# Gate logits of a gated DeltaNet layer as float32 products in four column groups, and its first decay rows spread by TensorE

## The chip, the core and the metric

The kernel runs on one core of one Trainium2 chip. The core has a matrix engine (TensorE, PE in the rows), a vector engine (VectorE, DVE), a scalar engine (ScalarE, ACT), GpSimd (POOL) and a queue that issues DMA transfers (SyncE, SP). Each engine works through its own instructions in a fixed order and waits on semaphores for the others. The metric is the device time of one execution in microseconds; lower is better.

## The reference

A prompt of 512 tokens and 8 groups of 4 sample tokens go through two layers; each layer is half an FFN, a mixer, and half an FFN, all on one residual stream. The second (odd) layer's mixer is a gated DeltaNet. Cut to what the change touches:

```python
def macaron_layer(x, mixer, n1, w1i, w1o, nm, n2, w2i, w2o):
    x = x + 0.5 * swiglu(rms_norm(x, n1), w1i, w1o)
    m, new_state = mixer(rms_norm(x, nm))
    x = x + m
    return x + 0.5 * swiglu(rms_norm(x, n2), w2i, w2o), new_state

def deltanet_mixer(u, conv_buf, S0, w_in, conv_w, A_log, dt_bias, o_gain, w_out):
    proj = u @ w_in                       # 1024 x 4112: q, k, v, z (1024 each), 8 + 8 logits
    qkv, z, b_logit, a_logit = jnp.split(proj, [...], axis=-1)
    qkv, new_buf = causal_conv(conv_buf, qkv, conv_w)
    q, k, v = jnp.split(jax.nn.silu(qkv), 3, axis=-1)     # 8 heads of 128, q and k normalized
    beta = jax.nn.sigmoid(b_logit)
    g = -jnp.exp(A_log) * jax.nn.softplus(a_logit + dt_bias)
    o, S = gated_delta_chunked(q, k, v, beta, g, S0)
    ...

def gated_delta_chunked(q, k, v, beta, g, S0):
    G = jnp.cumsum(gc, axis=-1)                           # within a chunk
    decay = jnp.exp(jnp.where(incl, G[..., :, None] - G[..., None, :], -jnp.inf))
    A = jnp.where(strict, jnp.einsum('bnhcd,bnhsd->bnhcs', kc, kc) * decay, 0.0) * bc[..., None]
    sol = lax.linalg.triangular_solve(A, rhs, ...)
    P = jnp.einsum('bnhcd,bnhsd->bnhcs', qc, kc) * decay
    ...                                                   # then a scan over the chunks
```

## The kernel before

The residual stream lies turned: 8 tiles x[k] of 128 features by 544 tokens (512 of the prompt, 32 samples), in float32. Beside each stands a pair xh, xl: the tile times the norm's gain, split in a rounded part and its rest. A large product (`mm3`, lines 367 to 369) is three products of such parts, wh xh + wh xl + wl xh, added up in an accumulator "lin" over the 8 feature tiles, once for 256 tokens and once for 288. Of "lin" there are two in the odd mixer. The norm's factor rstd is multiplied in only when VectorE empties the accumulator, so the products need not wait for the norm. A weight tile (`W`) is loaded by SP into one of two "raw" buffers, split by ScalarE (wh, line 328, three buffers) and VectorE (wl, line 329, two buffers).

The odd mixer begins with `norm_stats`: the sums of squares over the features are products with a matrix of ones (lines 288, 289), and rstd follows on ScalarE and VectorE. Then `odd_setup` makes beta and g for all tokens and heads. The 16 logits are a `mm3` with a weight of 16 columns: 48 products with 16 output rows. VectorE multiplies by rstd (bt, line 1043), TensorE turns bt to tokens by logits with five transposes (line 1047), and some twenty small VectorE instructions make g (line 1065). Products with triangles of ones sum it up to G (lines 1070 to 1074). G is turned once more (line 1098), copied (gt), written to DRAM (gdr) in five transfers, and read back into all partitions: grs for the samples (line 1105) and one "grow" per head (line 1160). `head_decay` makes from grow two decay matrices per head, Dn and Dt, in 16 VectorE instructions for two heads and some exponentials.

`odd_heads` works off a list of steps (`ODD_ORDER`, line 955): D decays, H the conv tiles of q and k and the products of a head (`head_stage`), B its values, V the triangular solve of two heads on VectorE (`solve`), Z the gate, L the levels that join the solved blocks (`levels`), C the chain over the chunks (`chain`), S and R the samples, O and M the output products. Two heads form a group. A conv tile (`conv_tile`) is one `mm3`, whose result VectorE copies times rstd into XP (lines 1120, 1123, 1124) and convolves in one ScalarE and three VectorE passes (lines 1132, 1134). `head_stage` squares q and k on ScalarE only for the sums; the squares themselves go to a scratch tile "junk". The tiles Dn, Dt, kt, qg and vb of all groups share 15 buffers of tag "st", in turn; accumulators of tag "m" are two.

A scheduler derives the order of each engine from the program and the dependences, and the whole odd mixer is ordered together; where instructions stand can be read only from the built program. `E.after` adds a dependence for the order alone.

## Time and profile before

| | us |
|---|---|
| median of 3 runs | 1911.97 (1911.93 to 1913.39) |
| the profiled execution | 1916.94 |
| its span, first to last instruction | 1915.2 |
| TensorE busy | 1861.2 (97%) |
| VectorE busy | 1078.1 (56%) |
| ScalarE busy | 836.9 (44%) |
| mean granted clock of TensorE | 0.991 of 2.4 GHz |

The profile is of one execution. Times within it count from the span's start. The last FFN of the layer ahead ends near 1197 us and the odd mixer fills the time to about 1610 us. Products are pipelined: one shown as 0.29 us starts 0.12 to 0.13 us behind the one ahead, at the full clock.

### The profile page before, as it was taken

The page shows a single profiled execution, that of the slowest core. Times are in us where ns is not written, and L with a number is a line of the kernel's source. Part 1 is how long each engine was busy: PE and PEld are TensorE (multiplying, and loading weights), DVE is VectorE, ACT ScalarE, POOL GpSimd, SP SyncE. Part 2 cuts the span into 40 slices and gives each one's busy share as a digit, 9 for nine tenths or more (in the row PEclk, how much of TensorE's full clock was granted, in tenths as well). Part 3 has the DMA queues.
Part 4 walks back from the last instruction along what each step waited for, and adds up shares of the span by engine and source line. Part 5 has one row for each costly group of instructions (what it writes and reads, how often), then busy time and mean ns, then how long its engine had stood idle before and what let it go on. Part 6 is the DMA issues. An engine that isn't in the chain of part 4 may idle for free.

```text
span 1915.2 us, 36694 instructions
## 1 busy us (share of the span) xinstructions
PE 1861.2 (97%) x15101; PEld 1793.0 (94%) x15101; DVE 1078.1 (56%) x2565; ACT 836.9 (44%) x1733; POOL 121.2 (6%) x229
## 2 busy tenths in 40 slices
PE   7999999999999999999999999899998999999999
PEld 6999999889777999999999999799997998999998
DVE  7444335776856444433544433688978877444422
ACT  6333224777755333323333322466675646333221
POOL 0000002111430000000000000111111100000000
PEclk9999999999999999999999999899999999999999
DMA  4323333222431333333332322333343332333232
GB/s 131 86 85 89 87 89 99 76 59 76 141 100 58 89 89 89 89 89 93 90 87 86 88 81 80 87 88 95 99 124 76 94 95 65 89 88 86 81 112 68
DMA packets 315973, 171.05 MB, mean 89 GB/s; under 512 B 28470, under 2 KB 310278, under 8 KB 315804
## 3 DMA queue, kind: packets, MB, share of 16 engines
q1 hardware_dynamic: 313244, 160.30, 29.5%
q0 software_dynamic: 2560, 8.39, 1.5%
q8 instruction: 119, 1.95, 0.4%
q14 instruction: 50, 0.41, 0.1%
HBM read 158.01 MB, written 10.65 MB: 88 GB/s over the span
## 4 chain that ended last, share of the span: by engine, by line
PE 58%; DVE 5%; ACT 2%; issue 1%; DMA 1%; POOL 0%; SPq 0%; ACTq 0%; DVEq 0%; POOLq 0%
PE lin L367 18%; PE lin L368 17%; PE lin L369 17%; DVE acc L1134 1%; DVE wl L329 1%; DVE LT L1252 1%; DVE ltmp L1251 1%; PE s L1479 0%; DMA raw<-in_w_in_odd 0%; PE m L1211 0%; DMA raw<-in_w_ffn_in 0%; ACT wh L328 0%; DVE Dn L1165 0%; PE c L1349 0%; DMA grs<-gdr 0%
## 5 line engine op out<-in xcount | busy, mean ns | idle before, releaser
L367 PE MATMUL lin<-xh,wh 128*128 128x256 f32 (+2 forms) x2992 | 875.0, 293 | 20.0 <-DVE XP L1120 5.0
L368 PE MATMUL lin<-xl,wh 128*128 128x256 f32 (+2 forms) x2992 | 870.5, 291 | 1.4 <-DVE xl L376 0.7
L369 PE MATMUL lin<-xh,wl 128*128 128x256 f32 (+2 forms) x2992 | 865.8, 290 | 0.5 <-DVE wl L329 0.5
L367 PEld LDWEIGHTS lin<-xh,wh 128*128 128x128 f32 (+1 forms) x2992 | 565.6, 189 | 25.7 <-ACT wh L328 6.4
L368 PEld LDWEIGHTS lin<-xl,wh 128*128 128x128 f32 (+1 forms) x2992 | 566.1, 189 | 3.9 <-DVE xl L273 1.5
L369 PEld LDWEIGHTS lin<-xh,wl 128*128 128x128 f32 (+1 forms) x2992 | 566.8, 189 | 2.6 <-issue 0.8
L328 ACT ACTIVATE wh<-raw 128x1024 fp32r<-128x1024 f32 x261 | 275.8, 1057 | 492.1 <-PE lin L368 419.2
L329 DVE TENSOR_TENSOR wl<-raw,wh 128x1024 fp32r<-128x1024 f32 x261 | 317.2, 1215 | 89.9 <-PE lin L369 88.0
L367 PE MATMUL lin<-hh,wh 128*128 128x288 f32 (+1 forms) x1024 | 295.7, 289 | 0.0
L368 PE MATMUL lin<-hl,wh 128*128 128x288 f32 (+1 forms) x1024 | 295.4, 288 | 0.0
L369 PE MATMUL lin<-hh,wl 128*128 128x288 f32 (+1 forms) x1024 | 294.9, 288 | 0.0
L368 PEld LDWEIGHTS lin<-hl,wh 128*128 128x128 f32 x1024 | 193.0, 188 | 0.2
L369 PEld LDWEIGHTS lin<-hh,wl 128*128 128x128 f32 x1024 | 192.7, 188 | 0.1
L367 PEld LDWEIGHTS lin<-hh,wh 128*128 128x128 f32 x1024 | 192.5, 188 | 0.1
L406 DVE TENSOR_TENSOR sg<-lin,rstd 128x256 f32<-128x256 f32 (+1 forms) x128 | 55.9, 438 | 162.1 <-PE lin L369 162.1
L375 ACT ACTIVATE hh<-pr 128x256 fp32r<-128x256 f32 (+1 forms) x128 | 55.1, 431 | 204.1 <-DVE pr L412 203.9
L411 DVE TENSOR_TENSOR pr<-lin,rstd 128x256 f32<-128x256 f32 (+1 forms) x128 | 56.5, 441 | 155.2 <-PE lin L369 155.1
L428 DVE SCALAR_TENSOR_TENSOR x<-lin,x 128x256 f32<-128x256 f32 x64 | 28.2, 441 | 168.7 <-PE lin L369 168.7
L376 DVE TENSOR_TENSOR hl<-pr,hh 128x256 fp32r<-128x256 f32 (+1 forms) x128 | 56.6, 442 | 61.2 <-ACT hh L375 61.2
L100 ACT ACTIVATE sg<-sg 128x256 f32<-128x256 f32 (+1 forms) x128 | 53.7, 422 | 55.9 <-DVE sg L406 55.9
L272 ACT ACTIVATE xh<-x,vec 128x544 fp32r<-128x544 f32 (+2 forms) x64 | 39.6, 631 | 71.5 <-DVE x L428 59.3
L1134 DVE SCALAR_TENSOR_TENSOR acc<-XP,cw,acc 128x568 f32<-128x568 f32 x72 | 58.8, 817 | 2.5 <-ACT acc L1132 2.2
(492 smaller groups left out, 2068.7 us busy)
## 6 DMA issues: line engine op xcount, KB each, us to landing
raw<-in_w_ffn_in SPq DMA_DIRECT2D x128, 512.0 KB
raw<-in_w_ffn_out SPq DMA_DIRECT2D x64, 512.0 KB
raw<-in_w_in_odd SPq DMA_DIRECT2D x32, 512.0 KB
raw<-in_w_in_even SPq DMA_DIRECT2D x20, 512.0 KB
raw<-in_w_out_even SPq DMA_DIRECT2D x8, 512.0 KB
S<-in_state_dn_S SPq DMA_DIRECT2D x8, 512.0 KB
out_dn_S_sample<-S SPq DMA_DIRECT2D x8, 512.0 KB
raw<-in_w_out_odd SPq DMA_DIRECT2D x8, 512.0 KB
```

Of the source, the lines that this page charges most:

```text
L100: i = self.nc.scalar.activation(out, in_, func, **kw).ins
L272: nc.scalar.activation(xh, x, AF.Copy, scale=g)
L328: nc.scalar.activation(self.h, raw, AF.Copy)
L329: nc.vector.tensor_tensor(self.l, raw, self.h.bitcast(F32), op=ALU.subtract)
L367: nc.tensor.matmul(ps[:n], lhsT=wh, rhs=rh, start=(i == 0), stop=False)
L368: nc.tensor.matmul(ps[:n], lhsT=wh, rhs=rl, start=False, stop=False)
L369: E.last_mm = nc.tensor.matmul(ps[:n], lhsT=wl, rhs=rh, start=False, stop=(i == len(terms) - 1)).ins
L375: nc.scalar.activation(yh, src, AF.Copy)
L376: nc.vector.tensor_tensor(yl, src, yh.bitcast(F32), op=ALU.subtract)
L406: nc.vector.tensor_tensor(s, ps, E.rstd[:, c0:c0 + cn], op=ALU.mult)
L411: nc.vector.tensor_tensor(p_, ps, E.rstd[:, c0:c0 + cn], op=ALU.mult)
L1134: nc.vector.scalar_tensor_tensor(a, XP[:, j:j + XW - 3], cw[j], a, op0=ALU.mult, op1=ALU.add)
```

## The change

The 16-column weight is loaded in the middle of the FFN ahead (`odd_consts`), padded with zeros to 32 columns and multiplied by the norm's gain on VectorE (bw). In `odd_setup` the logits are float32 products of bw with x itself, not with xh and xl: feature tile 4i + j goes to the 32 output rows 32j to 32j + 31, so four groups of 32 columns of the array hold four partial sums, and 16 products replace 48. `E.after` orders each of them behind the last product of the norm. The sum over the four groups is made while turning: the transposes become products with bsum, four stacked 16 x 16 unit matrices. Three constants (tri, stri, sones) are loaded at the mixer's start into a scratch tile.

grs, and the rows of G for heads 0 and 1, no longer come through DRAM: products with a column of the unit matrix, repeated 128 times, as weights put one row of gt into all partitions. ScalarE copies grs out; the decays of the two heads read the rows in the accumulators "c" and "z". gdr is still written, and read for heads 2 to 7. The "junk" tiles go: the squares are written to kt, kw or vb.

```diff
 def rsqrt_half(E, h, out, sq, ones, width, sh, sl, y):
-    nc.tensor.matmul(ps, lhsT=ones, rhs=sl, start=False, stop=True)
+    E.norm_mm = nc.tensor.matmul(ps, lhsT=ones, rhs=sl, start=False, stop=True).ins
...
-def odd_consts(E, op):
+def odd_consts(E, op, w_in):
...
-    E.tri = const("c_tri", [P, P])
-    E.stri = const("c_stri", [NS, NS])
-    E.sones = const("c_sones", [NS, NS])
+    E.bw = op.tile([P, KD, 32], F32, name="bw")
+    nc.vector.memset(E.bw, 0.0)
+    nc.sync.dma_start(out=E.bw[:, :, :16], in_=w_in[:, 4096:4112].rearrange("(k p) c -> p k c", p=P))
+    for k in range(KD):
+        nc.vector.tensor_scalar(E.bw[:, k], E.bw[:, k], col(E, "norm_mix", KD + k), None, op0=ALU.mult)
+    E.bsum = op.tile([P, 16], F32, name="bsum")
+    nc.vector.tensor_tensor(E.bsum, E.ident[:, 0:16], E.ident[:, 32:48], op=ALU.add)
+    for j in (2, 3):
+        nc.vector.tensor_tensor(E.bsum, E.bsum, E.ident[:, 32 * j:32 * j + 16], op=ALU.add)
...
 def odd_setup(E, op, sp, w_in):
-    w = W(E, w_in[:, 4096:4112])
...
-    def ev(h, c0, cn, ps):
-        nc.vector.tensor_tensor(bt[:16, c0:c0 + cn], ps[:16], E.rstd[:16, c0:c0 + cn], op=ALU.mult)
-    mm3(E, [w], E.xh, E.xl, ev)
+    for (c0, cn), tag in zip(HALVES, ("z", "pv")):
+        ps = cps(E, [P, cn], tag)
+        for i in range(2):
+            for j in range(4):
+                mm = nc.tensor.matmul(ps[32 * j:32 * j + 32], lhsT=E.bw[:, 4 * i + j], rhs=E.x[4 * i + j][:, c0:c0 + cn], start=(i == 0), stop=(i == 1), skip_group_check=True)
+                E.after(mm.ins, E.norm_mm)
+        nc.vector.tensor_tensor(bt[:, c0:c0 + cn], ps, E.rstd[:, c0:c0 + cn], op=ALU.mult)
+    cst = E.f()
+    tri, stri, sones = cst[:, :P], cst[:NS, P:P + NS], cst[:NS, P + NS:P + 2 * NS]
+    for t, key in ((tri, "c_tri"), (stri, "c_stri"), (sones, "c_sones")):
+        nc.sync.dma_start(out=t, in_=E.I[key])
     ps = E.m([P, 5, 16])
     for t, (c0, n) in enumerate(TOKS):
-        nc.tensor.transpose(ps[:n, t], bt[:16, c0:c0 + n], E.ident[:16, :16])
+        nc.tensor.matmul(ps[:n, t], lhsT=bt[:, c0:c0 + n], rhs=E.bsum, start=True, stop=True)
...
     E.grs = op.tile([P, NH, NS], F32, name="grs")
-    nc.sync.dma_start(out=E.grs, in_=E.gdr[:, T:].unsqueeze(0).to_broadcast([P, NH, NS]))
+    row = lambda r: E.ident[:40, r:r + 1].to_broadcast([40, P])
+    ps = cps(E, [P, NH, NS], "s")
+    for h in range(NH):
+        nc.tensor.matmul(ps[:, h], lhsT=row(32 + h), rhs=gt[:40, :NS], start=True, stop=True)
+    nc.scalar.activation(E.grs, ps, AF.Copy)
+    E.growps = [cps(E, [P, 4, P], t) for t in ("c", "z")]
+    for h, ps in enumerate(E.growps):
+        for c in range(4):
+            nc.tensor.matmul(ps[:, c], lhsT=row(8 * c + h), rhs=gt[:40, :P], start=True, stop=True)
...
 def head_decay(E, op, h):
-    nc.sync.dma_start(out=grow, in_=E.gdr[h:h + 1].to_broadcast([P, NT]))
+    if h < GH:
+        src = E.growps[h]
+    else:
+        nc.sync.dma_start(out=grow, in_=E.gdr[h:h + 1].to_broadcast([P, NT]))
+        src = ch(grow)
...
 def head_stage(E, op, w_in, h, H, ssq, adr, sq):
+    kt = op.tile([P, 4, P], F32, tag="st", name=E.nm("kt"), bufs=ST)
     pq = E.m([P, 4, P])
...
-        nc.scalar.activation(E.junk[0], pq[:, c], AF.Square, accum_out=ssq[:, gi, c:c + 1])
-    kt = op.tile([P, 4, P], F32, tag="st", name=E.nm("kt"), bufs=ST)
+        nc.scalar.activation(kt[:, c], pq[:, c], AF.Square, accum_out=ssq[:, gi, c:c + 1])
...
-        nc.scalar.activation(E.junk[0], pk[:, c], AF.Square, accum_out=ssk[:, c:c + 1])
+        nc.scalar.activation(kt[:, c], pk[:, c], AF.Square, accum_out=ssk[:, c:c + 1])
...
 def chain(E, op, Hs, V, g0, ssq, sz, yy, cuts=(4,)):
-            nc.scalar.activation(E.junk[1], ot[:, c, h], AF.Square, accum_out=sso[:, h, c:c + 1])
+            nc.scalar.activation(Hs[h].vb[:, c], ot[:, c, h], AF.Square, accum_out=sso[:, h, c:c + 1])
```

The new order is seen at three places. First TensorE at the norm. In the rows, "lin" are the products of `mm3`, r is the split of the squares, z and pv are the accumulators of the new logits; before, the turning of bt stands right behind the last narrow product:

Before:

```order
L367 MATMUL lin_13130<-xh_8_92,wh_13099 16x288
L368 MATMUL lin_13130<-xl_16_100,wh_13099 16x288
L369 MATMUL lin_13130<-xh_8_92,wl_13100 16x288
L1047 MATMUL m_13156<-ident,bt_13103 128x16 x2
L367 MATMUL lin_13287<-xh_933_6636,wh_13280 128x256
L368 MATMUL lin_13287<-xl_934_6637,wh_13280 128x256
L369 MATMUL lin_13287<-xh_933_6636,wl_13281 128x256
L367 MATMUL lin_13287<-xh_935_6638,wh_13280 128x256
L1047 MATMUL m_13156<-ident,bt_13103 128x16 x2
L1047 MATMUL m_13156<-ident,bt_13103 32x16
```

And now:

```order
L288 MATMUL m_13086<-r_13081,onesr 128x256
L369 MATMUL lin_13303<-xh_935_6638,wl_13271 128x288
L367 MATMUL lin_13303<-xh_937_6640,wh_13270 128x288
L288 MATMUL m_13096<-r_13081,onesr 128x288
L289 MATMUL m_13086<-r_13082,onesr 128x256
L368 MATMUL lin_13303<-xl_938_6641,wh_13270 128x288
L289 MATMUL m_13096<-r_13082,onesr 128x288
L1052 MATMUL z_13105<-x_77,bw 32x256
L1052 MATMUL z_13105<-x_78,bw 32x256
L1052 MATMUL z_13105<-x_79,bw 32x256
L1052 MATMUL z_13105<-x_80,bw 32x256
```

The narrow products are gone. The first conv tile (lin_13303, 24 products of it done ahead) now stands around the norm's products, and the logits' products come behind the last of these; the turning of bt follows 12 products further on.

Second VectorE between G and the first decays (gt is the copy of G's turned rows, wl a weight split, acc a convolution pass, smba and smbp the samples' decays). Before:

```order
L1100 COPY gt_13225<-m_13223 40x128
L1088 TENSOR_TENSOR egl<-egl,G 128x40
L1134 SCALAR_TENSOR_TENSOR acc_13342<-XP_13284,cw,acc_13342 128x568
L329 TENSOR_TENSOR wl_13492<-raw_13489,wh_13491 128x1024
L1134 SCALAR_TENSOR_TENSOR acc_13342<-XP_13284,cw,acc_13342 128x568
L1120 TENSOR_TENSOR XP_13355<-lin_13358,rstd 128x256
L1134 SCALAR_TENSOR_TENSOR acc_13342<-XP_13284,cw,acc_13342 128x568
L1123 TENSOR_TENSOR XP_13355<-lin_13384,rstd 128x256
L1124 TENSOR_TENSOR XP_13355<-lin_13384,rstd 128x8x4
L329 TENSOR_TENSOR wl_13563<-raw_13560,wh_13562 128x1024
L1134 SCALAR_TENSOR_TENSOR acc_13413<-XP_13355,cw,acc_13413 128x568
L1387 TENSOR_TENSOR smba_13238<-grs,G 32x64
```

And now:

```order
L1114 COPY gt_13198<-m_13196 40x128
L1102 TENSOR_TENSOR egl<-egl,G 128x40
L1146 TENSOR_TENSOR XP_13485<-lin_13514,rstd 128x256
L1147 TENSOR_TENSOR XP_13485<-lin_13514,rstd 128x8x4
L329 TENSOR_TENSOR wl_13693<-raw_13690,wh_13692 128x1024
L1414 TENSOR_TENSOR smba_13230<-grs,G 32x64
L1414 TENSOR_TENSOR smbp_13234<-grs,G 32x64
L1415 TENSOR_TENSOR smba_13230<-smba_13230,c_smba 32x64
L1415 TENSOR_TENSOR smbp_13234<-smbp_13234,c_smbp 32x64
L1192 SCALAR_TENSOR_TENSOR Dn_13241<-c_13216,G,c_mba 128x128
```

Of what stood between gt and the decays, the convolution passes have moved ahead of g (six of them, with two weight splits), and the decays read grs and the accumulator c. Behind them, XP copies and passes follow as before.

Third ScalarE at head 3, whose sums of squares are in ssq_14511 before and ssq_14501 now (lv are copies in the levels of the first two heads, U and ot copies in their chain). Before:

```order
L1132 ACTIVATE acc_14981<-XP_14923,cw 128x568
L1186 ACTIVATE junk_13071,ssq_14511<-m_14989 128x128 x4
L100 ACTIVATE acc_14981<-acc_14981 128x512
L1278 ACTIVATE lv_13999<-c_14006 32x8x32
L1279 ACTIVATE lv_13999<-c_14006 32x8x32
L100 ACTIVATE sq_14510<-acc_14981 128x32
```

And now:

```order
L1388 ACTIVATE ot_14330<-pv_14382 128x256
L1545 ACTIVATE um_14487<-Ur_14281,c_bsel 96x128
L1390 ACTIVATE vb_13766,sso_14331<-ot_14330 128x128
L1390 ACTIVATE vb_13847,sso_14331<-ot_14330 128x128
L1373 ACTIVATE U_14395<-z_14390 128x256
L1214 ACTIVATE kt_14979,ssq_14501<-m_14980 128x128 x4
L1219 ACTIVATE kt_14979,ssk_14978<-m_14989 128x128 x2
```

The squares of head 3 stood just ahead of the levels' copies; now they stand behind the chain's U of the fourth chunk (U_14395), and write to kt_14979.

## Rows read from the trace of the kernel before

**Rows 1.** The page, span and part 1: busy us (share), instructions per engine

```profile
span 1915.2 us, 36694 instructions
PE 1861.2 (97%) x15101; PEld 1793.0 (94%) x15101; DVE 1078.1 (56%) x2565; ACT 836.9 (44%) x1733; POOL 121.2 (6%) x229
```

**Rows 2.** Waits of TensorE, 1196 to 1640: us in total, times, longest

```profile
PE lin L367 <- DVE XP L1120: 5.0, 2, 3.7
PE lin L367 <- DVE sz L1565: 4.5, 1, 4.5
```

**Rows 3.** Busy time by stage: us, each engine (instructions), PEclk, DMA share, GB/s

```profile
1197.40:1205.40 8.00, 7.13 (x54) 4.79 (x51) 3.94 (x6) 4.75 (x11) 1.49 (x5) 1.00 0.41 117
1205.40:1207.40 2.00, 0.07 (x2) 0.01 (x1) 1.88 (x6) 1.37 (x3) 0.00 (x0) 1.00 0.00 0
1208.50:1211.70 3.20, 3.20 (x18) 3.17 (x16) 2.08 (x11) 0.47 (x2) 0.95 (x1) 0.50 0.41 116
1229.60:1233.30 3.70, 0.03 (x1) 0.00 (x1) 3.70 (x13) 3.51 (x6) 0.00 (x0) 0.88 0.00 0
1233.30:1239.20 5.90, 5.87 (x27) 5.90 (x28) 2.71 (x8) 3.35 (x7) 3.17 (x5) 0.50 0.35 98
```

**Rows 4.** The chain that ended last, 1218 to 1228: start, us, what

```profile
1218.42 0.28 DVE gt L1100
...
1220.09 1.16 DMA gdr<-gt
...
1221.31 5.96 DMA grs<-gdr
```

**Rows 5.** Timeline of VectorE: start, us, engine, line, operation, shapes

```profile
1208.90 0.15 DVE L1051 COPY ba<-m 32x16 f32<-32x16 f32 x1
...
1215.59 0.20 DVE L1065 SCALAR_TENSOR_TENSOR g<-g,ad 128x40 f32<-128x40 f32 x1
...
1227.84 0.34 DVE L1165 SCALAR_TENSOR_TENSOR Dn<-grow,G,c_mba 128x128 f32<-128x128 f32 x1
...
1232.76 0.42 DVE L1120 TENSOR_TENSOR XP<-lin,rstd 128x256 f32<-128x256 f32 x1
```

**Rows 6.** Timeline of TensorE, like instructions merged (count at the end)

```profile
1241.38 1.16 PE L1203 MATMUL m<-acc 128*128 128x128 f32 x8
...
1285.94 0.63 PE L1455 MATMUL s<-sV,skw 32*128 32x32 f32 x4
...
1558.74 1.94 PE L1479 MATMUL s<-S,wqz 128*32 128x128 f32 x60
```

**Rows 7.** Timeline of ScalarE; in brackets idle time ahead and its releaser

```profile
1198.99 1.06 ACT L328 ACTIVATE wh<-raw 128x1024 fp32r<-128x1024 f32 x1 [3.62 <-DMA raw<-in_w_in_odd]
...
1202.24 0.75 ACT L285 ACTIVATE r<-xsq 128x256 fp32r<-128x256 f32 x2 [1.00 <-DVE xsq L278]
```

**Rows 8.** The page, part 5: busy us, mean ns of one | idle ahead

```profile
L329 DVE TENSOR_TENSOR wl<-raw,wh 128x1024 fp32r<-128x1024 f32 x261 | 317.2, 1215 | 89.9 <-PE lin L369 88.0
...
L1134 DVE SCALAR_TENSOR_TENSOR acc<-XP,cw,acc 128x568 f32<-128x568 f32 x72 | 58.8, 817 | 2.5 <-ACT acc L1132 2.2
```

**Rows 9.** Timeline of SP's queue: loads of the solved blocks, groups 0 and 2

```profile
1311.19 2.69 SPq L1270 DMA_DIRECT2D V<-tdr  x4
...
1392.27 1.94 SPq L1270 DMA_DIRECT2D V<-tdr  x4
```

**Rows 10.** Timeline of TensorE: first bulk of level products, groups 0 and 2

```profile
1316.35 0.69 PE L1276 MATMUL c<-ident,V 32*32 32x32 f32 x44
...
1398.40 0.69 PE L1276 MATMUL c<-ident,V 32*32 32x32 f32 x44
```

**Rows 11.** Busy time by stage, as in rows 3

```profile
1406.00:1413.00 7.00, 7.00 (x40) 6.54 (x39) 3.56 (x14) 3.56 (x12) 1.43 (x2) 0.53 0.04 16
1441.00:1445.50 4.50, 0.26 (x3) 0.00 (x0) 4.50 (x10) 2.51 (x5) 1.51 (x4) 0.84 0.00 2
1445.50:1450.50 5.00, 4.72 (x22) 4.72 (x23) 4.62 (x17) 2.34 (x8) 0.12 (x1) 0.50 0.28 79
```

19 lines of the change are left out of this document (9 added, 10 removed).

## The prediction

> **What bounds the kernel now.** I read the page first, then the waits of TensorE, then its busy time and clock by stage, then the timelines around the odd mixer's start. TensorE is busy for 97% of the span [rows 1], so only TensorE's work, its idle time and its slow clock can carry a gain; VectorE, at 56%, matters where TensorE waits for it. The longest waits of TensorE in the odd mixer are two for the copy that empties an accumulator into XP (5.0 us, 3.7 of them at once) and one for the same copy of a gate (4.5) [rows 2]. The stages show what the start costs [rows 3]. From 1197.4 to 1205.4 the 48 narrow products for the logits and four products of the norm run, 7.13 us busy. Then comes a gap of 1.93 us until rstd and the scaled logits are there. From 1208.5 to 1211.7 the granted clock is 0.50, the lower of its two levels. From 1229.6 to 1233.3 TensorE is empty, and for 5.9 us behind that the clock is 0.50 again. The second gap has its cause in the chain [rows 4]: G's turned rows are copied out of the accumulator at 1218.4, go out through SP and DMA, and are back in all partitions at 1227.3. The decays on VectorE wait for them, and behind the decays in VectorE's queue stands the XP copy that TensorE waits for, at 1232.76 [rows 5].
>
> **The change part by part.** All against the profiled execution, 1916.94 us (span 1915.2). The median of the runs is 4.97 us below it, and I carry the difference over to the median.
>
> *Removed on TensorE.* The stage with the narrow products has 54 instructions in 7.13 us, 0.13 each [rows 3]; 48 of them make 6.3. The gaps 0.87, 1.93 and 3.67 make 6.5. Of the time at the lower clock, 3.2 and 5.9 us, half comes back if TensorE isn't idle ahead of it: 4.5. Together 17.3.
>
> *Added on TensorE.* First 16 float32 products in four column groups; each float32 product is two instructions in the trace. The trace has this shape: 60 instructions of 128 columns into 32 output rows, the groups taken in turn, in 1.94 us, 0.032 apart [rows 6]. With 272 columns in the mean, 32 x 0.032 x 2.1 = 2.1 us. Full-width float32 instructions start 0.126 apart (1.16 us for eight, less 0.28 for the tail of the last) [rows 6]; if the groups did not overlap, the block would take 32 x 0.126 x 2.1 = 8.5. The row of 60 has the same tile shape, so I take 2.1 and keep 8.5 as a rival. The logits are turned by five true products instead of five transposes: at most five instructions more, 0.5. Eight products for grs are 16 instructions of 32 columns; the nearest row is 0.63 us for four, 0.12 apart [rows 6], so 1.9. Eight for the rows of the first two heads: 16 x 0.126 = 2.0. Together 6.5, with bounds of 5.5 and 13.
>
> On this block the Trainium skill (TensorE: Matmul & The Clock Gate, part 3 on packing small matmuls, "The mechanism") says that a weight load overlaps running products only when its row group differs; here all four groups use all rows. By that rule the block would be near the serial end, 8.5 us, and the gain 6.4 smaller. The row of 60, whose groups use all rows too, speaks against it.
>
> *New waits on TensorE.* Without the narrow products TensorE reaches the norm's products earlier. The norm is earlier too: before, ScalarE held back the last tile's xh behind a weight split that waited 3.62 us for its DMA [rows 7]; with the narrow weight gone that load and split are one place earlier, and ScalarE's copy r of the squares starts at about 1200.9 instead of 1202.24. About 0.4 us of waiting is left there. The order puts the first half of a conv tile ahead of the block and 12 products behind it, so rstd is covered. Two more waits of 0.4 us I expect at the second and third conv tile, whose accumulators now wait behind convolution passes on VectorE. Sum 1.2, bounds 0.4 and 4.
>
> TensorE's own sum is so 17.3 - 6.5 - 1.2 = 9.6 us.
>
> *The decays' chain* moves less. g is no longer made at once: the order puts two weight splits, six convolution passes and five XP copies ahead of it on VectorE. The logits were copied out at 1208.9 [rows 5]; rstd is 1.3 earlier, of which the products ahead of the turning take back about 0.5, so 1208.1. From there to g two splits of 1.2, six passes of 0.8 [rows 8], five copies of at most 0.4 and some 20 small instructions of 0.2 [rows 5]: 13.2 us end to end, and about 11.4 with each starting before the one ahead has ended, by 0.07 or more. So g is there at 1219.5, where it was at 1215.8. From g to G's turned rows 2.8 us as before [rows 4, 5]: 1222.3. Then no DMA, but 1.9 for grs and 1.0 for the first head's rows: decays from 1225.2, before 1227.84 [rows 5]. That is 2.6 us earlier, and VectorE has two passes and one XP tile more behind it (some 2.4 us). So the chain is about 5.0 us ahead, against TensorE's 9.6.
>
> *Edits at nothing.* The narrow weight's load, its memset, eight scalings and the three additions for bsum go into the middle of the FFN: a dozen VectorE instructions of some 0.2 us while TensorE runs products for 100 us; without that cover 2.4 us. The three constant loads go onto SP's queue behind LT, ahead of two weight loads that have several us of slack and far ahead of their own use at 1219; some 1 us if that slack is gone. The writes of G's rows stay for heads 2 to 7, behind nobody that TensorE waits for now. ScalarE's copy of grs, 0.4 us, lies beside the products for the heads' rows. Scratch tiles in place of junk cost no instruction; what they move is a rival below.
>
> **What the two sums make.** Where TensorE stays the bound it keeps 9.6; where it later waits for the solve of the first heads it keeps the chain's 5.0. The chain has little slack there: the last load of the solved blocks is issued at 1313.9 [rows 9] and the level products begin at 1316.35 [rows 10]. I take 7, between the two: 1911.97 - 7 = 1905.0.
>
> **The rivals.**
> *A. More comes back.* The 4.5 us that TensorE waits at 1441 for a gate's copy, with 5 us at half clock behind it [rows 11], come from the order on VectorE, where solve steps stand ahead of that copy; in the new order it stands ahead of the solve. If TensorE keeps 9.6 and 5 of these 7 us go as well: 14.6, so 1897.4. For it: the order. Against: decays and other copies stand ahead of it instead. Chance 0.13.
> *B. Given back.* The levels wait, and the narrow block or the products with 40 rows bring the clock down: behind a stretch of small products the trace has 7 us at 0.53 [rows 11], 3.3 us. From the chain's 5.0 that leaves 1.7; with half of it 3.4. So about 1909. For it: both occur in the trace. Against: small blocks elsewhere were followed by the full clock. Chance 0.20.
> *C. The column groups don't overlap:* 7 - 6.4 = 0.6, so 1911.4. Against: [rows 6]. Chance 0.06.
> *D. Slower.* The squares of head 3 wrote to junk; now they write to kt, whose buffer comes free only with the levels of the first two heads. On ScalarE they move from ahead of the levels to behind the third step of the chain; meanwhile the turned q holds one of the two "m" accumulators. This head's k k' products, and with them the second solve, start some 10 us later in TensorE's order. Before, the solved blocks' last load was issued at 1394.2 [rows 9] and the products began at 1398.40 [rows 10], so only 2 to 4 us are to spare. If TensorE waits 8 us there, with a slow stretch behind it (3.3), and 6 in the third solve: 7 - 17.3 = -10.3, so 1922. It decides from the point where both waits together exceed 7 us. For it: the order. Against: the solve itself has fewer other rows between its steps now. Chance 0.13.
>
> **How the numbers follow.** My forecast, a gain of 4.5 to 9 (1903 to 1907.5), gets the rest, 0.48. A measurement tells about 0.2%, 3.8 us, from no change. Faster by more: the forecast, A and a fifth of B, 0.65. Within: the rest of B, C and a fifth of D, 0.25. Slower: 0.10. The range leaves out the far half of A and nearly all of D, under 0.2 together: 1896.5 to 1914.5.
>
> **What would show it.** Right: the block on line 1052 takes 2 to 2.5 us; no gap of over 1 us between 1197 and 1232, and the full clock there; decays begin near 1225; the fourth conv tile ends some 9 us earlier. Wrong: the block takes 8 us; the clock is 0.50 behind it; TensorE waits at the levels of the first or second solve; or the gain stands at 1250 and is gone by 1600.

## The result, and the profile after

The changed kernel is slower: 1931.43 us in the median against 1912.62 for the kernel before on the same chip, a ratio of 1.0088 with a 95% interval of 1.0070 to 1.0106. (Ratios are estimated over the runs and can differ by 0.1% from the quotient of the medians.) The forecast was 1905.0, with a range of 1896.5 to 1914.5. The profiled execution took 1936.22 us and is the slowest of its six; a second profile of each kernel comes further down.

The page of the changed kernel, span and part 1, beside [rows 1]:

```profile
span 1934.5 us, 36738 instructions
PE 1873.3 (97%) x15122; PEld 1804.8 (93%) x15122; DVE 1076.9 (56%) x2576; ACT 831.7 (43%) x1733; POOL 119.8 (6%) x229
```

The span is 19.3 us longer than before and TensorE is busy 12.1 us longer, with only 21 instructions more. Most of the loss is therefore neither added work nor a wait of TensorE.

**The start, in this execution, does what was forecast.** The timeline of TensorE in the changed kernel, like instructions merged (start, us, line, count at the end), beside [rows 6]:

```profile
1202.18 1.07 PE L1052 MATMUL z<-x,bw 128*32 128x256 f32 x16
1203.07 1.15 PE L1052 MATMUL pv<-x,bw 128*32 128x288 f32 x16
...
1222.28 1.97 PE L1123 MATMUL s<-gt,ident 40*128 40x32 f32 x16
...
1224.09 1.13 PE L1128 MATMUL c<-gt,ident 40*128 40x128 f32 x8
1225.06 1.05 PE L1128 MATMUL z<-gt,ident 40*128 40x128 f32 x8
```

The logits' block ends 2.04 us after it begins (2.1 forecast), grs takes 1.97 (1.9), the rows of the two heads 2.0 (2.0). On VectorE g and the first decays, beside [rows 5]:

```profile
1219.01 0.20 DVE L1079 SCALAR_TENSOR_TENSOR g<-g,ad 128x40 f32<-128x40 f32 x1
...
1225.26 0.35 DVE L1192 SCALAR_TENSOR_TENSOR Dn<-c,G,c_mba 128x128 f32<-128x128 f32 x1
```

g was forecast for 1219.5 and the decays for 1225.2. SP's queue, the four loads of the solved blocks V, and TensorE's first products on the first two of them, beside [rows 9] and [rows 10]:

```profile
1302.94 1.78 SPq L1297 DMA_DIRECT2D V<-tdr  x4
...
1393.87 1.94 SPq L1297 DMA_DIRECT2D V<-tdr  x4
...
1482.30 2.06 SPq L1297 DMA_DIRECT2D V<-tdr  x4
...
1569.98 2.94 SPq L1297 DMA_DIRECT2D V<-tdr  x4
```

```profile
1307.38 0.69 PE L1303 MATMUL c<-ident,V 32*32 32x32 f32 x44
...
1399.22 0.69 PE L1303 MATMUL c<-ident,V 32*32 32x32 f32 x44
```

The third and fourth load in the kernel before, on the same queue:

```profile
1466.09 2.94 SPq L1270 DMA_DIRECT2D V<-tdr  x4
...
1553.20 3.79 SPq L1270 DMA_DIRECT2D V<-tdr  x4
```

The first levels begin 9.0 us earlier than before (1307.38 against 1316.35). The second begin 0.8 later, the third load is issued 16.2 later and the fourth 16.8. So the gain is there at 1307 and is gone 90 us on; another 16 us are lost by 1482.

**Where the time lies.** Busy time by stretch of the changed kernel (columns as in [rows 3]): the start, then the stretches behind the first and the second levels, and last "the window", from the end of the last product of the FFN ahead of the odd mixer to the first second-stage product of the last FFN. It holds the odd mixer and that FFN's first stage:

```profile
1197.30:1240.00 42.70, 41.83 (x345) 39.11 (x343) 34.64 (x106) 23.77 (x61) 11.24 (x24) 1.00 0.31 85
1316.30:1326.50 10.20, 10.20 (x51) 9.64 (x52) 4.19 (x17) 4.89 (x17) 1.82 (x4) 0.50 0.08 29
1405.10:1422.20 17.10, 16.89 (x124) 15.08 (x124) 5.96 (x19) 7.69 (x31) 2.02 (x2) 0.50 0.18 49
1197.33:1828.14 630.81, 601.68 (x5245) 574.37 (x5245) 431.21 (x1374) 316.94 (x847) 59.42 (x128) 0.96 0.32 86
```

The stretches behind the levels and the window of the kernel before:

```profile
1325.00:1335.00 10.00, 10.00 (x90) 9.64 (x89) 9.50 (x47) 9.28 (x34) 1.95 (x4) 1.00 0.11 30
1406.50:1413.30 6.80, 6.80 (x35) 6.12 (x35) 3.86 (x15) 3.53 (x12) 1.29 (x1) 0.50 0.07 25
1197.56:1809.14 611.58, 589.89 (x5224) 562.76 (x5223) 434.60 (x1375) 322.93 (x847) 60.93 (x128) 0.98 0.33 90
```

The start runs at the full clock with 0.87 us of TensorE empty in 42.7. Outside the window the executions agree: it begins at 1197.56 and 1197.33, and what follows it takes about 106 us in both. So all of the loss, 19.2 us, is in the window. Of this 3.2 us lie in the first stage of the last FFN: from the last product of its norm to the window's end it takes 189.3 us now and took 186.2. There TensorE waits 2.2 us for sg, the first scaled copy of an accumulator, since VectorE now has a weight split ahead of the norm's split. The other 16 us are in the mixer.

Two readings of the rows split the 19.2. TensorE's empty time (length less busy) rises from 21.7 to 29.1 us, 7.4 more. The rest is the lower clock: behind the first levels 10.2 us at 0.50 where before ran at 1.00, behind the second 17.1 where before had 6.8, with shorter ones further on. By the granted clock's rows 51 us of the window are at 0.50 where before had 24, of which 51 and 21 are busy; half of that is what the clock costs, 25.4 against 10.6, so 14.8 more. The two terms make 22.2, which leaves -3 for the work. That is an estimate, since the ends of products are modelled.

No single wait carries the 7.4. The longest after 1420, from the waits of TensorE (us in total, times, longest):

```profile
PE lin L367 <- DVE x L1614: 5.5, 6, 1.6
PE lin L367 <- DVE sz L1591: 2.6, 1, 2.6
PE lin L367 <- DVE sg L406: 2.2, 1, 2.2
```

The wait for the gate's copy, 4.5 us in [rows 2], is 2.6 now.

### The profile page after: what moved, and what is told of

Same layout as the page of the kernel before. It is cut to its first block, busy times and chain, and to the rows that moved or that the text cites. A ratio compares the mean times of both kernels' runs of the same rounds, so it can differ in the third digit from the quotient of the medians.

```text
span 1934.5 us, 36738 instructions
## 1 busy us (share of the span) xinstructions
PE 1873.3 (97%) x15122; PEld 1804.8 (93%) x15122; DVE 1076.9 (56%) x2576; ACT 831.7 (43%) x1733; POOL 119.8 (6%) x229
## 4 chain that ended last, share of the span: by engine, by line
PE 58%; DVE 5%; DMA 2%; ACT 1%; issue 1%; SPq 0%; DVEq 0%; ACTq 0%
PE lin L367 17%; PE lin L368 17%; PE lin L369 17%; DMA raw<-in_w_in_odd 1%; DVE acc L1157 1%; DVE wl L329 1%; PE s L1506 1%; DVE ltmp L1278 1%; DVE LT L1279 1%; PE z L1369 0%; PE c L1376 0%; PE c L1344 0%; PE pv L1387 0%; ACT wh L328 0%; DMA xsq<-gdr 0%
## 5 line engine op out<-in xcount | busy, mean ns | idle before, releaser
L367 PE MATMUL lin<-xh,wh 128*128 128x256 f32 (+1 forms) x2976 | 869.7, 292 | 15.4 <-DVE x L1614 4.7
L368 PE MATMUL lin<-xl,wh 128*128 128x256 f32 (+1 forms) x2976 | 865.9, 291 | 1.3 <-issue 0.8
L369 PE MATMUL lin<-xh,wl 128*128 128x256 f32 (+1 forms) x2976 | 862.4, 290 | 1.7 <-DVE wl L329 1.7
L367 PEld LDWEIGHTS lin<-xh,wh 128*128 128x128 f32 x2976 | 564.0, 190 | 20.1 <-DVE x L1614 6.0
L369 PEld LDWEIGHTS lin<-xh,wl 128*128 128x128 f32 x2976 | 565.8, 190 | 4.7 <-DVE wl L329 2.0
L368 PEld LDWEIGHTS lin<-xl,wh 128*128 128x128 f32 x2976 | 564.4, 190 | 2.8 <-issue 1.0
L329 DVE TENSOR_TENSOR wl<-raw,wh 128x1024 fp32r<-128x1024 f32 x260 | 316.7, 1218 | 90.0 <-PE lin L369 88.1
L412 DVE TENSOR_TENSOR pr<-pr,sg 128x256 f32<-128x256 f32 (+1 forms) x128 | 56.1, 439 | 6.9 <-ACT sg L100 0.5
```

The lines of the kernel that those rows point to most:

```text
L329: nc.vector.tensor_tensor(self.l, raw, self.h.bitcast(F32), op=ALU.subtract)
L367: nc.tensor.matmul(ps[:n], lhsT=wh, rhs=rh, start=(i == 0), stop=False)
L368: nc.tensor.matmul(ps[:n], lhsT=wh, rhs=rl, start=False, stop=False)
L369: E.last_mm = nc.tensor.matmul(ps[:n], lhsT=wl, rhs=rh, start=False, stop=(i == len(terms) - 1)).ins
L412: nc.vector.tensor_tensor(p_, p_, sg[:, c0:c0 + cn], op=ALU.mult)
```

## The experiments

Kernels that run together share the runs of the kernel before on that chip. Two theories stood at the beginning: **the scratch** (rival D of the prediction: squares that write to kt hold up heads 3, 5 and 7) and **the earlier start** (TensorE runs ahead of VectorE, and the clock falls behind small products wherever the squares go). A third came with the first results, **the order**: the changed dependences make the planner derive another order for the whole mixer, and that order is worse, whichever part of the change caused it.

### One part at a time

All of the change but the scratch tiles, the squares going to junk as before (f_LG; edit against the changed kernel):

```diff
-    kt = op.tile([P, 4, P], F32, tag="st", name=E.nm("kt"), bufs=ST)
     pq = E.m([P, 4, P])
...
-        nc.scalar.activation(kt[:, c], pq[:, c], AF.Square, accum_out=ssq[:, gi, c:c + 1])
+        nc.scalar.activation(E.junk[0], pq[:, c], AF.Square, accum_out=ssq[:, gi, c:c + 1])
+    kt = op.tile([P, 4, P], F32, tag="st", name=E.nm("kt"), bufs=ST)
...
-            nc.scalar.activation(Hs[h].vb[:, c], ot[:, c, h], AF.Square, accum_out=sso[:, h, c:c + 1])
+            nc.scalar.activation(E.junk[1], ot[:, c, h], AF.Square, accum_out=sso[:, h, c:c + 1])
```

> The changed kernel with its two scratch tiles for the squares put back; the new logits and the rows spread by TensorE stay. Theory 1 (the loss comes from the scratch: squares written to kt wait for a buffer of tag st, so the k k' products of heads 3, 5 and 7 and the solves behind them come late, TensorE waits and its clock falls): the lead of 10 us that the changed kernel has at 1313 us is mostly kept, the time is 1902 to 1908. Theory 2 (the loss comes with the earlier start: TensorE runs ahead of VectorE, reaches the levels and the samples' block at once, and the clock falls behind these small products, wherever the squares go): 1920 to 1935, with 8 us or more at half clock behind the first levels.

Measured: 1925.6 us, ratio 1.0032 (1.0017 to 1.0048). Then the scratch tiles alone (f_J), the same lines the other way round in the kernel before:

> The kernel before with one part of the change alone: the squares are written to kt, vb and kw in place of the two scratch tiles; logits, constants and decays as before. Theory 1: it is slower by the loss of the changed kernel and the gain that went with it: 1920 to 1940. Theory 2: it is the kernel before within 0.2%: 1908 to 1916.

Measured: 1929.4 us, 1.0060 (1.0040 to 1.0079). The logits' part alone (f_L: the float32 block, bsum and the constants loaded late; G's rows still by DMA):

```diff
-    mm3(E, [w], E.xh, E.xl, ev)
+    for (c0, cn), tag in zip(HALVES, ("z", "pv")):
+        ps = cps(E, [P, cn], tag)
...
+                mm = nc.tensor.matmul(ps[32 * j:32 * j + 32], lhsT=E.bw[:, 4 * i + j], ...)
+                E.after(mm.ins, E.norm_mm)
```

> The new logits alone (float32 products in four column groups, their weight loaded ahead, three constants in a scratch tile); scratch tiles, the samples' row and the rows of all heads through DRAM as before. Both theories: the 3.7 us gap ahead of the decays stays or moves, so it gains less than both parts together. Theory 1: 1905 to 1911. Theory 2: 1912 to 1925.

Measured: 1926.1 us, 1.0032 (1.0018 to 1.0047). And the rows spread by TensorE alone (f_G), the logits by narrow products as before:

```diff
-    nc.sync.dma_start(out=E.grs, in_=E.gdr[:, T:].unsqueeze(0).to_broadcast([P, NH, NS]))
...
+        nc.tensor.matmul(ps[:, h], lhsT=row(32 + h), rhs=gt[:40, :NS], start=True, stop=True)
...
+    E.growps = [cps(E, [P, 4, P], t) for t in ("c", "z")]
```

> The rows spread by TensorE alone; logits as 48 narrow products, scratch tiles as before. It takes the gap of 3.7 us and the half clock behind it (3) and adds 3.9 us of small products. Theory 1: 1907 to 1912. Theory 2: 1912 to 1920.

Measured: 1940.24 us, 1.0123 (1.0100 to 1.0146). Every part alone is slower than the kernel before, also the two that touch no scratch tile; f_G is slower than either theory allowed. By ratio f_LG lies between its two theories, and the lead that the first one wanted is gone: its first level products start 118.7 us after the mixer's start, against 116.5 and 116.2 in the two profiles of the kernel before. f_L and f_G have them at 118.8 and 122.9, although f_G's first decays come earlier (25.6 us after the mixer's start, 30.0 before; f_L's come later, at 33.2).

The scratch's 0.60% and the rest's 0.32% add up to the whole, but the parts of the rest don't add up: 0.32% and 1.23% give 0.32% together. A cost that depends in this way on which dependences are there speaks for the order. Nor are the losses of one kind. f_J's executions have the clock of the kernel before beside them (0.990 in the mean of both), and its profile has 29.7 us of empty time in the window where both profiles of the kernel before have 21.7: the scratch tiles alone lose by empty time. The changed kernel loses mostly by the clock (below).

### The order held

The rows of every engine in the mixer can be held to a given order by edges that wait for nothing on the chip and add no instruction:

```diff
         odd_setup(E, cp, op, w_in)
+        n0 = len(nc.cur_bb.bb.instructions)
         odd_heads(E, op, dp, w_in, w_out, nxt)
+        pin(E, n0, ())
```

pin gives each instruction of an engine an edge to the one that a list names as its forerunner. First f_LG in the order of the kernel before (p_new_old); then the kernel before in the order that was derived for f_LG (p_old_new):

> The new logits and the spread rows, with scratch tiles as before, and every engine's instructions from the first decays to the end of the mixer held in the order of the kernel before (order dependences alone; what is computed is the same). Only norm, logits, g and G may stand elsewhere. Theory 1 (the earlier start is worth what the trace shows at 1313 us, and the order that the scheduler derives anew behind it costs more): faster than before by 5 to 10 us, ratio 0.995 to 0.9975. Theory 2 (the start's gain is given back wherever the rest stands, since VectorE's solves end no earlier): within 0.2% of before, with longer waits of TensorE at the levels.

> The kernel before, with every engine's instructions from the first decays to the end of the mixer held in the order that they have in the kernel with new logits, spread rows and scratch tiles (the one that was 0.3% slower). Theory 1 (the order costs): slower than before by that kernel's 6 us and the start's 5 to 10 us on top, ratio 1.006 to 1.009. Theory 2: no slower than that kernel, ratio 1.000 to 1.004.

Measured: 1917.94 us, 0.9998 (0.9986 to 1.0010), and 1925.84 us, 1.0041 (1.0028 to 1.0054). With f_LG's 1.0032, the new order costs 0.3 to 0.4% with either code and the old order costs nothing with either. So **the order carries the loss of this version**. By their numbers both runs fit the second theory of their expectations, but its reason does not hold: with the new start in the old order the first load of V comes 110.2 us after the mixer's start, 4 us earlier than in the kernel before (114.2). The decays begin at 26.4 us instead of 30.0, though XP's copies still stand behind them on VectorE, and 3.84 us of TensorE's second gap stay.

What is gained there is given back in the last FFN, whose order was not held. Up to the last product of that FFN's norm p_new_old's window takes 418.4 us and the kernel before's 421.7; the first stage of the FFN takes 187.8 and 186.2, with the 2.2 us wait for sg.

The kernel before held to its own order was not run. TensorE, VectorE and ScalarE have as many instructions with pin as without (15122, 2576 and 1733 in f_LG and p_new_old).

The two kernels of the study once more on this chip:

> The changed kernel on the chip of these runs, so that its stages are compared with kernels that ran beside it: ratio 1.007 to 1.0106 as in the first result; the half clock behind the first and second levels again (5 to 17 us each).

> The kernel before on the chip of these runs, for its stages: ratio 1.000 within 0.2%; half clock near 1209, 1233, 1406 and 1444 us, some 24 us in all.

Measured: 1937.47 us, 1.0101 (1.0087 to 1.0116), and 1917.47 us, 1.0002 (0.9988 to 1.0016).

### How far along the order costs

The next kernels take the changed kernel's order up to a point and the old one from there on. The point is counted in the wide products of the projections. They all have the squares in junk, and VectorE's old order at the start of the last FFN, so that the wait of 2.2 us goes and the first stage takes 185.8 us. Edit against p_new_old: other lists, and one more call of pin behind the last FFN.

> The kernel with the new start and the whole order of the kernel before, and now also VectorE's order of the last FFN, where the wait of 2.2 us for sg came in. If that wait was the order of a weight split ahead of the norm's split r, it goes: 2 us less than without, ratio 0.998 to 0.9995, the mixer and the FFN's start some 4 us shorter than in the kernel before. Otherwise as without, 0.9998.

> The same, but the changed kernel's order is held only up to the products of the first head; from there on the order of the kernel before. Theory 1: the gap of 3.8 us ahead of an XP copy goes, first solve 3 to 6 us earlier than in the kernel before, ratio 0.9965 to 0.9985. Theory 2: 0.998 to 1.002.

> New logits, spread rows, scratch tiles as before. Held by order dependences: up to the levels of the first two heads the order of the changed kernel (whose first solve was loaded 9 us earlier, counted from the mixer's start), behind it the order of the kernel before, and on VectorE the last FFN's order of the kernel before. Theory 1 (the start is worth 5 to 9 us of the solves' chain, and what lost them in the changed kernel is the order behind it): 5 to 9 us faster than before, ratio 0.995 to 0.9975, with no waits of over 1 us at the levels. Theory 2 (given back anyway): 0.998 to 1.002.

> As the fastest kernel so far (new logits, spread rows, scratch tiles as before, on VectorE the last FFN's order of the kernel before), but the changed kernel's order is held further: up to the levels of heads 2 and 3, and the order of the kernel before only behind them. If the changed order loses in its second solve (153 to 189 us from the mixer's start before, 160 to 191 with the change) and behind the first levels: 3 to 8 us slower than that kernel, ratio 0.999 to 1.002. If it loses behind the second levels alone: 0.997 to 0.9985.

> The same with the changed kernel's order up to the levels of heads 4 and 5. If the third group loses, as heads 4 and 5's late products and a late third solve would have it: ratio 1.001 to 1.006. If what is lost comes with the last group, whose products of head 7 stand 76 conv products later in the changed kernel: no more than 0.1% above the run with the order held to the second levels.

Measured, with what each holds of the changed kernel's order and the mean granted clock of its executions (the kernel before beside the first three had 0.9916, beside the next two 0.9918):

| changed order up to | median us | ratio | interval | mean clock |
|---|---|---|---|---|
| nowhere (c_0) | 1909.96 | 0.9984 | 0.9973 to 0.9995 | 0.9902 |
| 200 products (c_200) | 1910.32 | 0.9988 | 0.9979 to 0.9997 | 0.9917 |
| 628, the first levels (c_628) | 1907.53 | 0.9975 | 0.9966 to 0.9984 | 0.9936 |
| 1015, the second levels (c_1015) | 1917.38 | 1.0028 | 1.0014 to 1.0042 | 0.9909 |
| 1392, the third levels (c_1392) | 1924.89 | 1.0052 | 1.0035 to 1.0069 | 0.9885 |
| all, with the scratch tiles (the changed kernel) | 1931.43 | 1.0088 | 1.0070 to 1.0106 | 0.9843 |

The new order does no harm up to the first levels: c_628 is faster than both kernels of the study, by 0.25% or 5.6 us in the medians against the one before (1913.10 beside it). Against c_0 on the same chip it is 2.4 us, with intervals that overlap. **The stretch between the first and the second levels loses most, 0.53% or 10 us**, more than either theory of c_1015 allowed; the next loses 0.24%. The last 0.36% come with the rest of the order, the last FFN's order and the scratch tiles together.

What the order of the stretch up to the second levels does is seen at heads 3 and 5, whose k k' products open the later solves. VectorE multiplies them by the decays; c_628, the first of these rows for heads 3 and 5:

```profile
1327.75 0.34 DVE L1232 SCALAR_TENSOR_TENSOR Dn<-m,cf,Dn 128x128 f32<-128x128 f32 x1
...
1397.09 1.12 DVE L1232 SCALAR_TENSOR_TENSOR Dn<-m,cf,Dn 128x128 f32<-128x128 f32 x4
```

The same of c_1015:

```profile
1345.92 0.60 DVE L1232 SCALAR_TENSOR_TENSOR Dn<-m,cf,Dn 128x128 f32<-128x128 f32 x2
...
1405.79 1.12 DVE L1232 SCALAR_TENSOR_TENSOR Dn<-m,cf,Dn 128x128 f32<-128x128 f32 x4
```

The second load of V, on SP's queue, in c_628:

```profile
1387.54 1.94 SPq L1297 DMA_DIRECT2D V<-tdr  x4
```

and in c_1015:

```profile
1396.60 1.94 SPq L1297 DMA_DIRECT2D V<-tdr  x4
```

With the new order held through this stretch head 3 is 18 us later, and head 5 and the second load are 9 later; 3.4 us of each lie ahead of the mixer in these two executions, which the runs do not explain. The window, c_628:

```profile
1196.21:1800.56 604.35, 585.69 (x5245) 559.31 (x5245) 433.26 (x1374) 322.27 (x847) 59.49 (x128) 0.99 0.33 90
```

and c_1015:

```profile
1199.58:1809.39 609.81, 586.78 (x5246) 559.04 (x5245) 433.72 (x1374) 322.05 (x847) 61.62 (x128) 0.99 0.33 89
```

c_1015's is 5.5 us longer, and 4.4 of these are empty time of TensorE (23.0 against 18.7). So about half of the 10 us is seen in the rows. The other half fits the clock of the executions without a profile: the two profiled ones had 0.992 each, but the means of the table differ by 0.0027, which is 5 us of 1915. That is an upper estimate, since TensorE is not busy in all of the time at the lower clock.

### The scratch

In the kernel before, with only the squares of q and k to kt (f_J1; o's and the samples' stay in junk):

```diff
-        nc.scalar.activation(E.junk[0], pq[:, c], AF.Square, accum_out=ssq[:, gi, c:c + 1])
+        nc.scalar.activation(kt[:, c], pq[:, c], AF.Square, accum_out=ssq[:, gi, c:c + 1])
```

> The kernel before with a part of the scratch change: only the squares of q and k go to kt; those of the chain and the samples keep the scratch tiles. If the wait of these squares for a buffer of tag st is what makes the scratch change slow, it has all of its loss: ratio 1.004 to 1.008, second to fourth solve 5 to 15 us late. If it is the other squares: 0.999 to 1.002.

Measured: 1931.35 us, 1.0100 (1.0084 to 1.0116). These two lines carry all of the 0.6% that the scratch tiles cost alone, and more. Is it the wait for kt on the chip, or the place that the rows get for its sake? The kernel before, squares to junk and so without that wait, in the order of f_J1 (p_J1ord):

> The kernel before, scratch tiles and all, with every engine's instructions from the first decays to the end of the mixer held in the order that they have where q's and k's squares go to kt. Nothing waits for a buffer here that did not before. If the loss of that kernel is in the order that the scheduler made of the wait (products of heads 3, 5 and 7 behind the levels): ratio 1.008 to 1.012, the same late solves. If it is the waiting itself at run time: 0.998 to 1.003.

Measured: 1946.68 us, 1.0152 (1.0122 to 1.0182). **The order alone costs as much and more**, with no wait for kt left. Why it costs 0.5% more than with the wait stays open; the two profiles have nearly the same empty time (32.9 and 31.0 us), but the mean clock of the executions is lower, 0.982 against 0.988. Squares to kt in the old order were not run, so the price of the wait itself is not known.

Then the other way: the squares of q are written in place in the accumulator pq and kt is taken behind them, so that q's squares wait for no buffer, in f_J1 (g_J1K) and in the changed kernel (g_K):

```diff
-        nc.scalar.activation(kt[:, c], pq[:, c], AF.Square, accum_out=ssq[:, gi, c:c + 1])
+        nc.scalar.activation(pq[:, c], pq[:, c], AF.Square, accum_out=ssq[:, gi, c:c + 1])
+    kt = op.tile([P, 4, P], F32, tag="st", name=E.nm("kt"), bufs=ST)
```

> The kernel before, with q's squares written back to the accumulator that they are read from, and kt allocated behind them as before; k's squares go to kt. The wait of q's squares for a buffer of tag st is gone. If that wait is the cause: heads 5 and 7 come as early as in the kernel before, ratio 1.000 to 1.005 (the order is still derived anew, which alone cost 0.3% in other kernels). If not: 1.007 to 1.012 as with both squares in kt.

> The changed kernel, with q's squares written back to their accumulator and kt allocated behind them; the rest of the change stays. If the wait for kt is the largest part of its loss: ratio 1.000 to 1.005 in place of 1.0088. If the start's products and their clock are: 1.007 to 1.011.

Measured: 1929.78 us, 1.0063 (1.0046 to 1.0080), and 1933.86 us, 1.0089 (1.0071 to 1.0107). Alone it takes back a third of f_J1's loss, between the two ranges of its expectation; in the full change it takes back nothing, so the theory that the wait of q's squares is the largest part of the loss falls. By its number g_K fits the other theory, the start's products and their clock; against that one stands c_0, which has the same start and loses nothing. ScalarE's timeline shows where the squares went. The kernel before, head 3:

```profile
1314.55 0.25 ACT L1186 ACTIVATE junk<-m 128x128 f32<-128x128 f32 x1
```

The changed kernel:

```profile
1336.59 0.37 ACT L1373 ACTIVATE U<-z 128x256 f32<-128x256 f32 x1
1336.85 0.27 ACT L1214 ACTIVATE kt<-m 128x128 f32<-128x128 f32 x1
```

And g_K, first q's squares, then k's:

```profile
1310.10 0.26 ACT L1213 ACTIVATE m<-m 128x128 f32<-128x128 f32 x1
...
1346.73 0.26 ACT L1219 ACTIVATE kt<-m 128x128 f32<-128x128 f32 x1
```

q's squares go back to where they were, but k's, which write to kt also, now stand at 1346.7, and head 3's products by the decays are at 1352.30, 9 us later than in the changed kernel, 5 of them behind the mixer's start. The place was not won, it moved one step on. A kernel with the scratch tiles and one buffer more of that kind was not tried.

### The same program twice

> The kernel with the new start and the order of the kernel before, profiled once more: its first profiled execution was its slowest (1920 us beside a median of 1910) and showed 24 us at half clock behind the levels of the first and third heads' groups. If that clock is what sets its executions apart, an execution near 1910 shows full clock there and a mixer 8 to 10 us shorter (604 to 606 us in place of 613.9). If not, the same half clock at 1910.

Measured: 1915.45 us, 0.9986 (0.9974 to 0.9999), like c_0. The kernel was run again, on another chip, for its clock. Its first profiled execution, 1920.14 us, was the slowest of 13, and its mean clock of 0.983 the lowest (the others had 0.988 to 0.993); the stretches behind the first and the second levels, and the window:

```profile
1322.00:1332.20 10.20, 10.20 (x52) 9.65 (x52) 5.67 (x34) 6.20 (x18) 0.89 (x4) 0.50 0.07 28
1407.40:1421.10 13.70, 13.70 (x74) 12.79 (x74) 7.09 (x30) 7.09 (x22) 1.29 (x1) 0.50 0.16 47
1197.98:1811.86 613.88, 594.72 (x5247) 568.71 (x5245) 431.57 (x1374) 323.33 (x847) 59.68 (x128) 0.97 0.32 88
```

The second, 1909.83 us:

```profile
1322.70:1332.90 10.20, 10.20 (x91) 9.83 (x92) 9.38 (x52) 9.84 (x35) 0.73 (x3) 1.00 0.12 36
1403.40:1417.10 13.70, 13.41 (x120) 12.43 (x118) 11.83 (x41) 12.02 (x42) 1.30 (x1) 1.00 0.38 111
1198.67:1801.54 602.87, 583.07 (x5246) 557.51 (x5245) 433.42 (x1374) 322.28 (x847) 58.91 (x128) 0.99 0.33 90
```

The same instructions in the same order get 0.50 behind the levels in one execution and 1.00 in the other, and the window differs by 11.0 us.

The second profile of the changed kernel (after_again, the fastest of its four executions): the stretch at the end of the spread rows and behind them, then from 345 us after the mixer's start to the window's end, then the window:

```profile
1230.60:1237.40 6.80, 6.80 (x32) 6.58 (x31) 5.93 (x19) 4.76 (x10) 0.30 (x1) 0.50 0.25 70
1547.23:1821.88 274.65, 263.17 (x2175) 256.57 (x2175) 148.57 (x352) 101.28 (x209) 0.57 (x1) 0.97 0.29 83
1202.23:1821.88 619.65, 592.28 (x5247) 565.98 (x5245) 430.77 (x1374) 316.29 (x847) 60.87 (x128) 0.98 0.32 88
```

The kernel before beside it (before_again), from 345 us on and the window:

```profile
1546.73:1809.71 262.98, 258.50 (x2180) 250.63 (x2179) 144.06 (x331) 103.47 (x211) 0.57 (x1) 1.00 0.30 87
1201.73:1809.71 607.98, 586.30 (x5225) 559.34 (x5224) 435.54 (x1375) 322.76 (x847) 60.97 (x128) 0.99 0.33 91
```

From 345 us on in the first pair, the changed kernel and then the kernel before:

```profile
1542.33:1828.14 285.81, 272.34 (x2240) 264.61 (x2240) 157.49 (x384) 106.88 (x220) 2.02 (x3) 0.97 0.29 81
1542.56:1809.14 266.58, 262.14 (x2207) 254.12 (x2206) 147.81 (x342) 104.40 (x213) 0.57 (x1) 1.00 0.30 87
```

The window is 619.65 us here and was 630.81 in the first profile. These two profiles are 11.7 us apart where the first two were 19.2, and the medians 20.0 and 18.8. The slow clock behind the first and the second levels, which the expectation wanted again, is not there in this execution. In its place 6.8 us at the end of the spread rows and behind them have it, as in c_628. The first levels' bulk begins 5.1 us earlier than in the kernel before, counted from the mixer's start, where the first pair had 8.7.

What both pairs show lies behind 345 us. In the second pair TensorE has as many instructions left there in both kernels, 2175 and 2180, so about all of the 11.7 us are lost behind that point. TensorE is empty for 11.5 us there instead of 4.5 (first pair 13.5 and 4.4), and the clock's rows have 17 us at 0.50 in each profile of the changed kernel and none in either of the kernel before. The fourth load of V stands in this part, 11.6 us late in the second pair, and so does the wait for sg, 2.2 us in both. Split as above, the 11.7 us are 5.7 more empty time and 8.5 for the clock, less 2.5 for the work.

The runs without a profile agree on the clock. On the chip of the second pair the kernel before had a mean clock of 0.986 to 0.994 in 33 executions, 0.990 in the mean; the changed kernel had 0.980 to 0.985 in four, 0.982 in the mean (in the first result 0.981 to 0.988 in six). The difference is some 16 us of 1915, an upper estimate again, beside a loss of 20.0. So the lower clock is most of the loss in the median too. What brings it down more often in this order is not shown. Some 10 us between two single profiles are within what executions of one program differ by, and only the medians of several runs carry the verdict.

## Why the prediction was wrong

**Right: the terms of the start, with some luck in the execution.** The block took 2.04 us, so rival C (its groups don't overlap) falls, and with it, for this block, the rule on row groups that the prediction took from the Trainium skill (TensorE: Matmul & The Clock Gate, part 3 on packing small matmuls, "The mechanism"): all 32 instructions use all rows, and their two halves together end in 2.04 us, where the serial end was 8.5. grs, the rows, g at 1219.0 and the decays at 1225.3 came within 0.5 us. In the first profile the clock is full from 1197 to 1240 and TensorE is empty for 0.87 us in all. In the second, 6.8 us at the end of the spread rows and behind them have the lower clock, so the part of "half comes back" that stood for the 5.9 us behind the second gap did not come back there. The first levels' bulk begins 8.7 us earlier in the first pair and 5.1 in the second, so the chain's sum of 5.0 holds in the second pair and TensorE's 9.6 in neither quite.

**Wrong: "I take 7, between the two".** This step let the gain of the start run through to the end, and put the order that is derived behind the start at nothing; only B and D priced what it might move. With the old order behind it the start is worth 3 us (c_0, 0.16%), with the new order up to the first levels 0.25%, 4.8 us by the ratio (c_628): at the lower of the two ends that the step weighed, 5.0. The missing term is the derived order's cost. All ten kernels whose mixer was derived anew or held to such an order throughout lose 0.3 to 1.5%; in the changed kernel the loss is 0.88%, 18.8 us in the medians, so some 22 us against the start's 3. That it is the order is shown for f_LG (p_new_old and p_old_new); for the scratch p_J1ord shows that the order alone costs as much. For f_L, f_G and the changed kernel as a whole it is argued from these.

**Rival D named the late heads, but not how the time is lost.** It named head 3's squares and their move behind the chain's third step. The rows of its chain, VectorE's products of k k' with the decays for heads 3, 5 and 7, before:

```profile
1332.30 0.35 DVE L1205 SCALAR_TENSOR_TENSOR Dn<-m,cf,Dn 128x128 f32<-128x128 f32 x1
...
1401.60 1.12 DVE L1205 SCALAR_TENSOR_TENSOR Dn<-m,cf,Dn 128x128 f32<-128x128 f32 x4
...
1500.13 1.13 DVE L1205 SCALAR_TENSOR_TENSOR Dn<-m,cf,Dn 128x128 f32<-128x128 f32 x4
```

and after:

```profile
1343.28 0.60 DVE L1232 SCALAR_TENSOR_TENSOR Dn<-m,cf,Dn 128x128 f32<-128x128 f32 x2
...
1431.12 1.12 DVE L1232 SCALAR_TENSOR_TENSOR Dn<-m,cf,Dn 128x128 f32<-128x128 f32 x4
...
1514.79 1.12 DVE L1232 SCALAR_TENSOR_TENSOR Dn<-m,cf,Dn 128x128 f32<-128x128 f32 x4
```

Head 3 is 11 us later, as D said ("some 10 us"). Heads 5 and 7, which D did not price, are 30 and 15 later (22 and 10 in the second pair). But the second solve is hardly late: its levels begin 0.8 us later than before, and "waits 8 us there" and "6 in the third solve" are no waits of that size in the rows. The empty time comes at the end instead, 5.5 and 4.4 us between 345 and 380 us after the mixer's start where the kernel before has 0.3 both times. D gave 10.3 us slower; the median is 18.8. That its sign came out right is in part luck, since its waits did not occur and the slow clock that did most of it was one stretch of 3.3 us in D.

**Rival B had the other half.** It put the lower clock behind small products at 3.3 us in all; against the kernel before the clock costs 14.8 us more in the first pair and 8.5 in the second. Where it falls is a matter of the execution, how much of it there is in the median is not: the changed kernel's executions have 0.980 to 0.988. The step "small blocks elsewhere were followed by the full clock" read one execution as if it were the rule.

**Rival A** (more comes back) moved as it said and by less: the gate's wait went from 4.5 to 2.6 us, not to zero.

**"Scratch tiles in place of junk cost no instruction; what they move is a rival"** is right as it stands, but the chance of 0.13 was not. By f_J and f_J1 they alone cost 0.6 and 1.0%, and D did not need the rest of the change at all. The forecast also left out that the start's two parts would be slower each by itself.

**What stays open.** Which rows of the derived order cost, beyond the lateness of heads 3, 5 and 7: g_K has another place for head 3's squares and the same loss, and f_G, with no scratch tile moved, loses 1.23%. What brings the clock down in more of the executions under the new order is open too. The changed kernel itself, scratch tiles and all, was not run in the old order.

## What to carry to other kernels

Where a planner derives the order of a whole stage, an edit at its start re-derives the rest as well: hold the old order by edges behind the edited part, and measure edit and order apart. Here the same edits gave 1.0032 in the derived order, 0.9998 in the old one, 0.9984 with the old order of the next FFN held as well, and 0.9975 with the new order up to the first levels and the old one from there on. Take a second profile of the same program before a slow stretch is put down to the code, and set the mean clock of all executions beside the times. Scratch output that goes to a tile of a rotating buffer brings a wait where there was none, so look in the order how far it moves its instruction and, above all, what the same rule does to every later user of that buffer.

## What the runs showed of the hardware

Where the clock falls behind small products differs between executions of one program: in c_0, 10.2 us behind the first levels ran at 0.50 in one execution and at 1.00 in another, and 13.7 us behind the second levels did the same. Half of these 23.9 us is 12, about the 11.0 by which the two windows differ. How much falls in the mean differs between programs: with the same chip and nearly the same work, the kernel before had a mean clock of 0.986 to 0.994 in 33 executions and the changed kernel 0.980 to 0.985 in four.

The block of 32 float32 instructions in four column groups, 256 and 288 columns each, overlaps fully: the first 16, of 256 columns, start 0.056 us apart (0.89 us from the first half's start to the second's). Full-width instructions of 128 columns start 0.126 apart [rows 6], so twice the columns would be 0.25 apart, an estimate; the block takes about a quarter of it. The row of 60 with 128 columns in [rows 6] had 0.032.
